# Modulation weights multiplied on VectorE in the gating stage of a two-layer trunk kernel

## The chip, the cores and the metric

The kernel runs on one core of a Trainium2 chip. The metric is the device time of one execution in microseconds (us), lower is better. The engines carry the profile's names: PE is TensorE (matmuls), PEld its weight loads, DVE is VectorE, ACT is ScalarE, POOL is GpSimd, SP is the engine that issues most DMA transfers, in the order of its queue.

## What is computed

A trunk of two layers over 1024 latent tokens and 256 context tokens of width 1024. Layer 0 joins a recurrent branch (RG-LRU) and a spatial gating unit; layer 1 joins a gated convolution and differential attention. Around both stands the adaptive modulation, which the change is about:

```python
def modulation(cond, w, b):
    m = jax.nn.silu(cond) @ w + b                       # w: 1024 x 3072, one for each layer
    shift, scale, gate = jnp.split(m[:, None, :], 3, axis=-1)
    return shift, scale, gate

for l in range(DEPTH):                                  # two layers
    shift, scale, gate = modulation(c, w_mod[l], b_mod[l])                # latent tokens
    shift_c, scale_c, gate_c = modulation(c_ctx[None], w_mod[l], b_mod[l])  # context tokens
    h = x * (1.0 + scale) + shift
    hc = ctx * (1.0 + scale_c) + shift_c
    ...                                                 # y, yc from the layer's branches
    x = layer_norm(DEEPNORM_ALPHA * x + gate * y, ln_g[l], ln_b[l])
    if need_ctx_out:                                    # layer 0 only
        ctx = layer_norm(DEEPNORM_ALPHA * ctx + gate_c * yc, ln_g[l], ln_b[l])
```

There are two conditioning vectors, `c` and `c_ctx`, so each modulation is a product of a 2 x 1024 matrix with a 1024 x 3072 one. The 3072 columns are worked off in six blocks of 512 columns a layer: blocks 0 and 1 are the shift, 2 and 3 the scale, 4 and 5 the gate. The context's gate of layer 1 is not needed.

## The kernel before, in words

Matmuls with f32 accuracy are made of three passes: both operands are split into a high and a low part (`hi`, `lo`; ScalarE makes the first, GpSimd mostly the second), and three of the four products are summed. The kernel goes through these stages, times on the profile's clock:

- **Start** (to about 52 us): shift and scale of layer 0 and the modulated inputs. The change leaves it as it is.
- **Recurrent stage** (to about 232 us): four blocks of 128 channels. `lru_x` and `lru_g` are projections, `lru_rec` the gate matmuls (`pgate`) with ScalarE's activations, `lru_scan` the recurrence on VectorE, whose result goes to DRAM (`ya_d`). The rest of the modulation is done here, in eight blocks: `mod_load` loads eight weight tiles of 128 x 512 (`wm`), and `mod_step`, which stands between the parts of the stage and acts on every third call, does with `mod_do` the sixteen passes of one block (`modp`, L221) and the end of the block before: for shift and scale four transposes (`modcp`, L228) and sums on VectorE (`mod_cols`), for gates one matmul with a column selector (`gatep`, L494), the bias and a store to DRAM (`gate_d`).
- **Gating stage** (to about 367 us): the v projection by ten tiles of 128 tokens (`sgu_v`, tile `pv`) with a normalisation of each on VectorE (`vf`), the spatial matmuls (`sgu_s`, tile `sps`) that take two or three normalised tiles at a time between the matmuls of a later `pv`, and u and z projections of four channel groups (`pu`, `pz`). The first group's z and the second's u come at its beginning, the second group's z after the tiles, and then u and z of the third and of the fourth.
- **Output of layer 0**, then layer 1: projections, attention, output.

Each engine works off its instructions in program order. That order is the kernel's scheduler's, apart from some stretches on SP that are written by hand; a buffer of a pool (`bufs=n`) is given out again when the last reader of its old tile is done, and memory of a pool that was closed goes to later pools under the same condition.

Of the kernel before, what the change touches and what calls it, by code (L numbers as in the profile page):

```python
# [10 lines left out]
F32 = mybir.dt.float32  # L11
# [20 lines left out]
    ("slng", 4), ("slnb", 4), ("lng0", 8), ("lnb0", 8), ("sconv", 12), ("subln", 1), ("sel", 2),  # L32
# [10 lines left out]
def tile_hybrid_trunk(es: ExitStack, tc: tile.TileContext, A, out, scr=None):  # L43
# [48 lines left out]
    V.memset(cm05, -0.5)  # L92
    csil = const.tile([128, KT, 32], F32, name="csil")
# [272 lines left out]
    with pool("lrua") as lp, pool("lruc") as lc:  # L366
# [28 lines left out]
        def lru_g(f):  # L395
            if f:
                p = pj3("pg")
                PROJ(proj3c_g(p, wload(A["w_in0"][4 + f])))
            else:
                p = pg0  # L400
# [5 lines left out]
        def lru_rec(f):  # L406
            (wh, wl), = wload(A["wg"][f], nk=4)
            mod_step()
            xl, xh, xo = XL[f]
            bs = []  # L410
            for d in range(2):
# [22 lines left out]
                mod_step()  # L434
# [28 lines left out]
        def mod_load():  # L463
            if not blocks:
                return
            l, blk = blocks.pop(0)
            wm = {}
            for k in range(8):
                w = lp.tile([128, 512], F32, name="wm", tag="wm", bufs=8)
                SY.dma_start(w, A["w_mod"][l][128 * k:128 * k + 128, 512 * blk:512 * blk + 512])  # L470
                wm[k] = w
            pend.append((l, blk, wm))

        def mod_do():
            if late:
                mod_c(*late.pop(0))
            if pend:
                l, blk, wm = pend.pop(0)
                p = psb("modp")
                mod_mm(p, wm, range(8))  # L480
# [793 lines left out]
```

## Time and profile before

| | us |
|---|---|
| median of three runs | 1142.44 |
| the three runs | 1144.62, 1142.44, 1142.17 |
| the profiled execution | 1142.67 |
| its span in the trace | 1140.8 |
| PE busy | 1117.0 (98%) |
| DVE busy | 721.7 (63%) |
| ACT busy | 435.4 (38%) |
| POOL busy | 285.2 (25%) |
| granted TensorE clock, mean | 0.998 |

All durations below come from the one profiled execution. Its span leaves out 1.9 us around the traced instructions. Busy shares are means over stages with different limits; what an instruction costs is read from its stage, from the engine that is waited for there.

### The profile page before, as it was taken

To read this page: it belongs to the slowest core of one execution; us is meant where nothing else is said; L and a number is where in the kernel's file an instruction comes from. 1 tells how busy PE (TensorE), PEld (TensorE's weight loads), DVE (VectorE), ACT (ScalarE), POOL (GpSimd) and SP (SyncE) were. 2 spreads that over 40 slices of the span, in tenths; PEclk is the share of its full clock that TensorE was granted. 3 is DMA by queue.
4 is the path that set the end of the run, shared out by engine and by line. 5 is a ranking of instruction groups with operands and counts; after the bars stand their busy time and mean duration, and the time that the engine had idled before them with its cause. 6 is when DMAs were issued, how large, how long until landed. Compare 5 with 4: busy or idle time off the path is not lost.

```text
span 1140.8 us, 14960 instructions
## 1 busy us (share of the span) xinstructions
PE 1117.0 (98%) x5842; PEld 920.2 (81%) x5842; DVE 721.7 (63%) x1031; ACT 435.4 (38%) x681; POOL 285.2 (25%) x228
## 2 busy tenths in 40 slices
PE   6999999999999999999999999999999999999997
PEld 4777777878888888888888788888888888888886
DVE  5777986944412566637512776767676666738996
ACT  3463665620221243343212545445544444423210
POOL 0011112630240222258402322322421321220021
PEclk9999999999999999999999999999999999999999
DMA  9644543220241543336736242441522520127641
GB/s 367 258 172 164 185 151 108 94 97 1 75 145 61 174 149 125 114 123 211 240 93 177 96 121 72 114 119 62 144 94 47 137 99 20 47 70 238 217 146 69
DMA packets 78198, 148.08 MB, mean 130 GB/s; under 512 B 6304, under 2 KB 35872, under 8 KB 77232
## 3 DMA queue, kind: packets, MB, share of 16 engines
q1 hardware_dynamic: 71088, 128.25, 32.6%
q0 software_dynamic: 7040, 18.88, 7.4%
q8 instruction: 46, 0.75, 0.3%
q14 instruction: 24, 0.20, 0.1%
HBM read 112.49 MB, written 34.62 MB: 129 GB/s over the span
## 4 chain that ended last, share of the span: by engine, by line
PE 85%; DVE 4%; issue 3%; ACT 3%; POOL 2%; DMA 2%; POOLq 0%; SPq 0%; DVEq 0%; ACTq 0%
PE pout L681 6%; PE pout L683 6%; PE pout L682 6%; PE p L184 5%; PE p L186 5%; PE p L185 5%; PE pv L208 3%; PE pv L210 3%; PE pv L209 3%; PE psc L990 3%; PE psc L991 3%; PE atr L1013 3%; PE modp L221 2%; PE pav L1025 2%; PE pav L1027 2%
## 5 line engine op out<-in xcount | busy, mean ns | idle before, releaser
L141 POOL TENSOR_TENSOR wlo<-wraw,whi 128x512 fp32r<-128x512 f32 x86 | 133.5, 1556 | 427.8 <-ACT whi L138 427.7
L992 DVE TENSOR_REDUCE st<-psc 128x1 f32<-128x1280 f32 x64 | 95.0, 1485 | 39.6 <-PE psc L991 39.6
L681 PE MATMUL pout<-woh,yhi 128*128 128x512 f32 (+1 forms) x296 | 114.7, 387 | 0.1
L683 PE MATMUL pout<-woh,ylo 128*128 128x512 f32 (+1 forms) x296 | 114.4, 386 | 0.0
L682 PE MATMUL pout<-wol,yhi 128*128 128x512 f32 (+1 forms) x296 | 114.1, 385 | 0.0
L994 ACT ACTIVATE e<-psc,st 128x1280 f32<-128x1280 f32 x64 | 85.1, 1330 | 71.9 <-DVE st L992 69.1
L138 ACT ACTIVATE whi<-wraw 128x512 fp32r<-128x512 f32 x92 | 57.4, 627 | 125.1 <-PE px L173 26.9
L184 PE MATMUL p<-hhl,whi 128*128 128x512 f32 x256 | 105.0, 410 | 0.0
L186 PE MATMUL p<-hhl,wlo 128*128 128x512 f32 x256 | 100.5, 393 | 0.0
L185 PE MATMUL p<-hll,whi 128*128 128x512 f32 x256 | 100.3, 392 | 0.0
L138 ACT ACTIVATE ah<-atr 128x512 fp32r<-128x512 f32 (+1 forms) x96 | 47.0, 524 | 64.3 <-PE atr L1013 63.9
L990 PE MATMUL psc<-k,qh 128*128 128x512 f32 (+1 forms) x192 | 67.1, 364 | 2.6 <-ACT e L994 2.5
L991 PE MATMUL psc<-k,ql 128*128 128x512 f32 (+1 forms) x192 | 68.7, 358 | 0.0
L681 PEld LDWEIGHTS pout<-woh,yhi 128*128 128x128 f32 x296 | 55.7, 188 | 11.8 <-DVE zt L644 0.5
L683 PEld LDWEIGHTS pout<-woh,ylo 128*128 128x128 f32 x296 | 55.6, 188 | 11.6 <-DVE ylo L141 0.2
L682 PEld LDWEIGHTS pout<-wol,yhi 128*128 128x128 f32 x296 | 55.7, 188 | 11.4
L138 ACT ACTIVATE yhi<-yraw 128x512 fp32r<-128x512 f32 x36 | 22.5, 631 | 107.7 <-PE pout L682 72.1
L141 DVE TENSOR_TENSOR al<-atr,ah 128x512 fp32r<-128x512 f32 (+1 forms) x96 | 54.4, 593 | 6.3 <-ACT ah L138 6.2
L186 PEld LDWEIGHTS p<-hhl,wlo 128*128 128x128 f32 x256 | 48.0, 188 | 10.8
L185 PEld LDWEIGHTS p<-hll,whi 128*128 128x128 f32 x256 | 48.3, 189 | 8.2
L184 PEld LDWEIGHTS p<-hhl,whi 128*128 128x128 f32 x256 | 48.2, 188 | 8.0
L208 PE MATMUL pv<-wvh,hhl 128*128 128x512 f32 x128 | 52.0, 406 | 0.0
(325 smaller groups left out, 2817.2 us busy)
## 6 DMA issues: line engine op xcount, KB each, us to landing
wraw<-in_w_in_dram SPq DMA_DIRECT2D x42, 512.0 KB, 3.8
wm<-in_w_mod_dram SPq DMA_DIRECT2D x64, 256.0 KB, 4.4
wraw<-in_w_out_dram SPq DMA_DIRECT2D x16, 512.0 KB, 4.4
wm<-in_w_mod_dram SPq DMA_DIRECT2D x7, 1024.0 KB, 11.5
xt<-in_xcT_dram SPq DMA_DIRECT2D x8, 640.0 KB, 8.2
xres<-in_xc_dram SPq DMA_DIRECT2D x10, 512.0 KB, 3.6
wvr<-in_w_v_dram SPq DMA_DIRECT2D x8, 512.0 KB, 3.6
n_d<-xres SPq DMA_DIRECT2D x8, 512.0 KB, 2.6
```

The costliest lines, as they stand in the source:

```text
L138: S.activation(hi, src, AF.Copy)
L141: le.tensor_tensor(lo, src, f32(hi), op=ALU.subtract)
L184: T.matmul(o, hi[:, k % 4], hh[:, k], start=k == 0, stop=False)
L185: T.matmul(o, hi[:, k % 4], hl_[:, k], start=False, stop=False)
L186: T.matmul(o, lo[:, k % 4], hh[:, k], start=False, stop=k == KT - 1)
L208: T.matmul(p, hh[:, k], wh, start=k == 0, stop=False)
L681: T.matmul(o, hi[:, i], wh[:, c], start=first and i == 0, stop=False)
L682: T.matmul(o, hi[:, i], wl[:, c], start=False, stop=False)
L683: T.matmul(o, lo[:, i], wh[:, c], start=False, stop=not first and i == 3)
L990: T.matmul(o, qh[:, m, cu], KS[hd, m][:, c:c + n], start=True, stop=False)
L991: T.matmul(o, ql[:, m, cu], KS[hd, m][:, c:c + n], start=False, stop=True)
L992: V.tensor_reduce(st[:, m:m + 1], p[:, 256:1536], axis=AX.X, op=ALU.max, negate=True)
```

## The change

The whole block of modulation work leaves the recurrent stage. `mod_sums`, a generator, takes its place: for each of the eight blocks it loads the eight weight tiles one by one through three buffers, and VectorE multiplies a tile with the conditioning of its 128 rows (one number per partition), for the two conditioning vectors in turn, and adds it to an accumulator of 128 x 512 (`macc`). A block takes 16 such products, or 8 for the two blocks of which one conditioning is needed: 112 in all, 14 scalings (L237) and 98 multiply-adds (L239). `mod_rows` then lets TensorE sum the accumulator over the partitions: for shift and scale by eight matmuls with a column of ones, one column each (L253), for a gate by one matmul of 512 columns per conditioning (L260). The generator is called forward in the gating stage by `mod_step(n)`, which counts products: 5 (three tiles, six products) in each `sgu_v`, 12 after the second group's z, 14 after each later u and z, and all that is left after the fourth u. The sums of a block are issued when the fourth tile of the next block has been multiplied. One of the six `vf` buffers is given up.

```diff
+    sel = const.tile([128, 3], F32, name="sel")
+    V.memset(sel, 1.0)
+    V.memset(sel[:, 1:2], 0.0)
...
-    sel = P("sel")
-
-    def mod_cols(mb, out, bias, one):
-        p = psb("modcp")
-        for i in range(4):
-            T.transpose(p[:, 128 * i:128 * i + 128], mb[:, 128 * i:128 * i + 128], ident)
-        t = const.tile([128, 4, 2], F32, name="mct", tag="mct", bufs=2)
-        V.tensor_reduce(t, p.rearrange("p (i g r) -> p i r g", g=4, r=32)[:, :, 0:2, :], axis=AX.X, op=ALU.add)
-        for o, i0, i1, b, add in zip(out, (0, 2), (2, 4), bias, one):
-            V.scalar_tensor_tensor(o, t[:, i0:i1, :], add, b[:, :, None].to_broadcast([128, i1 - i0, 2]),
+    def mod_sums(mw):
+        blocks = [(1, i) for i in range(4)] + [(0, 4), (0, 5), (1, 4), (1, 5)]
+        late = None
+        for l, blk in blocks:
+            conds = 1 if (l, blk // 4) == (1, 1) else 2
+            acc = mw.tile([128, 2, 512], F32, name="macc", tag="macc", bufs=2)
+            for k in range(KT):
+                w = mw.tile([128, 512], F32, name="wm", tag="wm", bufs=3)
+                SY.dma_start(w, A["w_mod"][l][128 * k:128 * k + 128, 512 * blk:512 * blk + 512])
+                for c in range(conds):
+                    if k == 0:
+                        V.tensor_scalar(acc[:, c], w, csil[:, k, c:c + 1], None, op0=ALU.mult)
+                    else:
+                        V.scalar_tensor_tensor(acc[:, c], w, csil[:, k, c:c + 1], acc[:, c], op0=ALU.mult, op1=ALU.add)
+                if k == 3 and late is not None:
+                    mod_rows(mw, *late)
+                    late = None
+                yield conds
+            late = (l, blk, acc, conds)
+        mod_rows(mw, *late)
+
+    def mod_rows(mw, l, blk, acc, conds):
+        p = psb("modp")
+        if blk < 4:
+            s, j = divmod(blk, 2)
+            for i in range(4):
+                for c in range(2):
+                    T.matmul(p[:, 2 * i + c:2 * i + c + 1], acc[:, c, 128 * i:128 * i + 128], onesm[:, 0:1],
+                             start=True, stop=True)
+            V.scalar_tensor_tensor(mod1[:, 4 * j:4 * j + 4, s, :], p[:, 0:8].rearrange("p (i c) -> p i c", c=2),
+                                   float(s), P("bmod1")[:, 4 * blk:4 * blk + 4][:, :, None].to_broadcast([128, 4, 2]),
                                    op0=ALU.add, op1=ALU.add)
+        else:
+            for c in range(conds):
+                T.matmul(p[0:2, :], sel[:, c:c + 2], acc[:, c], start=c == 0, stop=c == conds - 1)
+            br = mw.tile([2, 512], F32, name="br", tag="br", bufs=1)
+            SY.dma_start(br, A["b_mod"][l:l + 1, 512 * blk:512 * blk + 512].to_broadcast([2, 512]))
+            V.tensor_tensor(br, p[0:2, :], br, op=ALU.add)
+            SY.dma_start(gate_d[2 * l:2 * l + 2, 512 * (blk - 4):512 * (blk - 4) + 512], br)
 
...
 in lru_x and lru_g:
-                PROJ(proj3c_g(p, WX1 if f == 1 else wload(A["w_in0"][f])))
+                run(proj3c_g(p, WX1 if f == 1 else wload(A["w_in0"][f])))
...
 in lru_rec:
-            mod_step()
 for d in range(2):
-                mod_step()
...
-        def mod_load():
...
-        def mod_do():
...
-        def mod_c(l, blk, mb):
...
-        mod_load()
...
         rec3 = lru_rec(3)
-        while pend or late:
-            mod_do()
...
+    mw_cm = pool("modw")
+    modg = mod_sums(mw_cm.__enter__())
+
+    def mod_step(n):
+        while n > 0:
+            c = next(modg, None)
+            if c is None:
+                return
+            n -= c
+
...
         def sgu_v(t, between=None):
...
             VH[t] = vf
+            mod_step(5)
...
         SY.dma_start(yb_d[1], zt1)
+        mod_step(12)
...
         sgu_u(g, w)
+        mod_step(14)
...
         sgu_z(g, w)
+        mod_step(14 if g == 2 else 100)
```

What moves, at three places. The first is VectorE's order where the v projection begins. `zt` L551 is the z step of the first channel group, L459 the end of the last recurrence, and BN_STATS to `vf` the normalisation of token tiles 0 and 1. Before:

```order
L551 SCALAR_TENSOR_TENSOR zt_1639<-zt_1639,pz 128x1280
L459 SCALAR_TENSOR_TENSOR gt<-gt,sg 128x1024
L579 BN_STATS bs<-vf_1987 128x6
L580 BN_AGGR bs<-bs 128x2
L581 TENSOR_SCALAR bs<-bs 128x1
L583 TENSOR_SCALAR vf_1987<-vf_1987,bs 128x512
L579 BN_STATS bs<-vf_1988 128x6
L580 BN_AGGR bs<-bs 128x2
```

In the changed kernel the rows from the recurrence's end (L488) on are these; line numbers are those of the new file, where the statistics and `vf` are L563 to L567:

```order
L488 SCALAR_TENSOR_TENSOR gt<-gt,sg 128x1024
L237 TENSOR_SCALAR macc<-wm,csil 128x512 x2
L239 SCALAR_TENSOR_TENSOR macc<-wm,csil,macc 128x512 x8
L563 BN_STATS bs<-vf_1717 128x6
L239 SCALAR_TENSOR_TENSOR macc<-wm,csil,macc 128x512 x2
L564 BN_AGGR bs<-bs 128x2
L239 SCALAR_TENSOR_TENSOR macc<-wm,csil,macc 128x512 x2
L565 TENSOR_SCALAR bs<-bs 128x1
L239 SCALAR_TENSOR_TENSOR macc<-wm,csil,macc 128x512 x2
L237 TENSOR_SCALAR macc<-wm,csil 128x512 x2
L567 TENSOR_SCALAR vf_1717<-vf_1717,bs 128x512
L563 BN_STATS bs<-vf_1718 128x6
```

and the rows up to the normalisation of token tile 2 (`vf_1719`), the last that the first spatial matmuls read:

```order
L567 TENSOR_SCALAR vf_1718<-vf_1718,bs 128x512
L590 SCALAR_TENSOR_TENSOR Bt<-rsum,par,Bt 128x128 x2
L239 SCALAR_TENSOR_TENSOR macc<-wm,csil,macc 128x512 x2
L564 BN_AGGR bs<-bs 128x2
L239 SCALAR_TENSOR_TENSOR macc<-wm,csil,macc 128x512 x2
L565 TENSOR_SCALAR bs<-bs 128x1
L239 SCALAR_TENSOR_TENSOR macc<-wm,csil,macc 128x512 x2
L563 BN_STATS bs<-vf_1720 128x6
L567 TENSOR_SCALAR vf_1719<-vf_1719,bs 128x512
```

Thirty products now stand ahead of the normalisation of tile 2. The second place is SP's queue at the same time; the changed kernel has, from the four loads of v weights on:

```order
L199 DMA wvr<-in_w_v_dram 128x2x512 x4
L490 DMA ya_d<-gt 128x256
L270 DMA wraw<-in_w_out_dram 128x1024
L490 DMA ya_d<-gt 128x1024
L544 DMA wsr<-in_sgu_wT_dram 128x512
L546 DMA Bt<-in_sgu_b_dram 128x512
L234 DMA wm<-in_w_mod_dram 128x512 x3
L262 DMA br<-in_b_mod_dram 2x512
```

The first three weight tiles (`wm`) stand behind both stores of the last recurrence. The third is SP's queue at the third and fourth channel groups. Before, from the load of the fourth z's weights to that group's store of its result:

```order
L145 DMA wraw<-in_w_in_dram 128x1024
L239 DMA wraw<-in_w_out_dram 128x1024 x3
L646 DMA yb_d<-zt 128x1280
L722 DMA gc<-gate_d 128x512 x2
L646 DMA yb_d<-zt 128x1280
```

After, from the last two w_out loads of that stretch on:

```order
L270 DMA wraw<-in_w_out_dram 128x1024 x2
L264 DMA gate_d<-br 2x512
L234 DMA wm<-in_w_mod_dram 128x512
L262 DMA br<-in_b_mod_dram 2x512
L632 DMA yb_d<-zt 128x1280
L234 DMA wm<-in_w_mod_dram 128x512
L264 DMA gate_d<-br 2x512
L234 DMA wm<-in_w_mod_dram 128x512 x2
L262 DMA br<-in_b_mod_dram 2x512
L234 DMA wm<-in_w_mod_dram 128x512 x5
L711 DMA gc<-gate_d 128x512
L234 DMA wm<-in_w_mod_dram 128x512 x2
```

Here the rest of the weight tiles, the bias rows (`br`), the stores of the gate rows and the loads of the context's gate (`gc`) stand in one queue. On TensorE the last two gate sums stand between the fourth group's u and z:

```order
L175 MATMUL pu<-hhl,whi 128x512
L176 MATMUL pu<-hll,whi 128x512
L177 MATMUL pu<-hhl,wlo 128x512
L260 MATMUL modp<-macc,sel 2x512 x2
L175 MATMUL pz<-hhc,whi 128x256
L176 MATMUL pz<-hlc,whi 128x256
L177 MATMUL pz<-hhc,wlo 128x256
```

Nothing stood between these two projections before.

## Rows read from the trace of the kernel before

**Rows 1.** The page: busy time by engine, and the shares of the chain of waits

```profile
PE 1117.0 (98%) x5842; PEld 920.2 (81%) x5842; DVE 721.7 (63%) x1031; ACT 435.4 (38%) x681; POOL 285.2 (25%) x228
...
PE 85%; DVE 4%; issue 3%; ACT 3%; POOL 2%; DMA 2%; POOLq 0%; SPq 0%; DVEq 0%; ACTq 0%
```

**Rows 2.** Timeline of PE, recurrent stage: start us, us, engine, line, operation, tiles, shape, count

```profile
63.48 1.92 PE L221 MATMUL modp<-wm,csil 128*32 128x512 f32 x16
65.34 0.50 PE L172 MATMUL px<-hhl,whi 128*128 128x512 f32 x1
...
77.60 0.59 PE L494 MATMUL gatep<-mb,par 128*2 128x512 f32 x1
...
80.27 0.38 PE L172 MATMUL pg<-hhc,whi 128*128 128x256 f32 x1
...
114.53 0.60 PE L228 MATMUL modcp<-ident,mb 128*128 128x128 f32 x4
...
116.91 0.38 PE L419 MATMUL pgate<-xh,whi 128*128 128x258 f32 x1
...
191.84 0.29 PE L419 MATMUL pgate<-xh,whi 128*128 128x258 f32 x1
...
203.43 1.02 PE L494 MATMUL gatep<-mb,par 128*2 128x512 f32 x2
204.38 0.39 PE L172 MATMUL pz<-hhc,whi 128*128 128x256 f32 x1
```

**Rows 3.** Timeline of ACT, second channel block; in brackets the idle time and its releaser

```profile
118.97 1.34 ACT L423 ACTIVATE gt<-pgate,hb 128x1282 f32<-128x1282 f32 x1 [0.84 <-PE pgate L421]
```

**Rows 4.** Timelines of DVE and PE around the start of the gating stage

```profile
231.22 1.48 DVE L551 SCALAR_TENSOR_TENSOR zt<-zt,pz 128x1280 f32<-128x1280 f32 x1
232.62 2.16 DVE L459 SCALAR_TENSOR_TENSOR gt<-gt,sg 128x1024 f32<-128x1024 f32 x1
...
232.75 0.51 PE L208 MATMUL pv<-wvh,hhc 128*128 128x512 f32 x1 [0.60 <-DVE zt L551]
```

**Rows 5.** Timeline of PE later in the kernel, at a sum over partitions

```profile
691.85 0.95 PE L1039 MATMUL pms<-onesm,sq 128*128 128x1 f32 x8
692.66 0.48 PE L184 MATMUL p<-hhl,whi 128*128 128x512 f32 x1
```

**Rows 6.** Timeline of PE, first group of spatial matmuls

```profile
257.32 0.83 PE L591 MATMUL sps<-wsr,vf 128*128 128x128 f32 x6
```

**Rows 7.** Groups of DVE by line and form: busy us, mean ns | idle before

```profile
L732 DVE SCALAR_TENSOR_TENSOR xres<-xres,pout 128x512 f32<-128x512 f32 x20 | 13.7, 683 | 1.2 <-DMA xres<-in_xc_dram 0.8
...
L579 DVE BATCH_NORM_STATS2 bs<-vf 128x6 f32<-128x512 f32 x10 | 6.9, 694 | 27.2 <-ACT vf L577 27.2
L583 DVE TENSOR_SCALAR vf<-vf,bs 128x512 f32<-128x512 f32 x10 | 5.4, 545 | 5.0 <-POOL bs L582 4.9
```

**Rows 8.** Windows: busy us of PE, PEld, DVE, ACT, POOL; PEclk, DMA share, GB/s

```profile
260.00:280.00 20.00, 20.00 (x101) 16.69 (x101) 7.21 (x17) 1.79 (x3) 1.64 (x3) 1.00 0.00 0
1137.00:1138.00 1.00, 0.00 (x0) 0.00 (x0) 0.43 (x1) 0.00 (x0) 0.00 (x0) 0.50 0.36 141
```

**Rows 9.** Tile wm: us from issue to landing, 73 loads of all sizes

```profile
DMA to landing us min/median/max: 2.7/4.5/13.6
```

**Rows 10.** Timelines of SP's queue and of PE, third and fourth channel groups

```profile
332.62 9.76 SPq L239 DMA_DIRECT2D wraw<-in_w_out_dram  x3
...
350.60 3.04 SPq L722 DMA_DIRECT2D gc<-gate_d  x2
...
339.62 0.28 PE L172 MATMUL pu<-hhc,whi 128*128 128x256 f32 x1
...
353.36 0.28 PE L172 MATMUL pz<-hhc,whi 128*128 128x256 f32 x1
```

**Rows 11.** Timeline of PE at the start of the kernel, recurrent input projections

```profile
11.59 1.31 PE L164 MATMUL px<-hhl,whi 128*128 128x512 f32 x2
...
21.02 0.63 PE L164 MATMUL px<-hhl,whi 128*128 128x512 f32 x2
```

More of the change, by code (lines that the diff above doesn't have):

```diff
@@ L31 @@
     ("cc", 16), ("bmod0", 24), ("bmod1", 24), ("convw", 16), ("convb", 4), ("ba", 8), ("bx", 8), ("lam", 8),
-    ("slng", 4), ("slnb", 4), ("lng0", 8), ("lnb0", 8), ("sconv", 12), ("subln", 1), ("sel", 2),
+    ("slng", 4), ("slnb", 4), ("lng0", 8), ("lnb0", 8), ("sconv", 12), ("subln", 1),
 ]
@@ L397, in lru_g @@
                 p = pj3("pg")
-                PROJ(proj3c_g(p, wload(A["w_in0"][4 + f])))
+                run(proj3c_g(p, wload(A["w_in0"][4 + f])))
             else:
@@ L461, in lru_scan @@
                 SY.dma_start(ya_d[f][:, s0:s0 + n], y[:, c0:c0 + n])
-        def mod_load():
[L464 to L472, printed above, removed]
-        def mod_do():
[L475 to L480, printed above, removed]
-                mb = lp.tile([128, 512], F32, name="mb", tag="mb", bufs=1)
-                V.tensor_copy(mb, p)
-                late.append((l, blk, mb))
-                mod_load()
-        def mod_c(l, blk, mb):
-            if blk < 4:
-                s, j = divmod(blk, 2)
-                k0 = 4 * j
-                mod_cols(mb, [mod1[:, k0 + 2 * i:k0 + 2 * i + 2, s, :] for i in range(2)],
-                         [P("bmod1")[:, 4 * blk + 2 * i:4 * blk + 2 * i + 2] for i in range(2)], (float(s),) * 2)
-            else:
-                pg = psb("gatep")
-                T.matmul(pg[0:2, :], sel, mb, start=True, stop=True)
-                br = lp.tile([2, 512], F32, name="br", tag="br", bufs=1)
-                SY.dma_start(br, A["b_mod"][l:l + 1, 512 * blk:512 * blk + 512].to_broadcast([2, 512]))
-                V.tensor_tensor(br, pg[0:2, :], br, op=ALU.add)
-                SY.dma_start(gate_d[2 * l:2 * l + 2, 512 * (blk - 4):512 * (blk - 4) + 512], br)
-        blocks = [(0, 4), (0, 5)] + [(1, i) for i in range(6)]
-        late, pend, calls = [], [], [0]
-        def mod_step():
-            calls[0] += 1
-            if calls[0] % 3 == 2:
-                mod_do()
-        def interleave(gen):
-            for i, _ in enumerate(gen):
-                if i in (9, 17):
-                    mod_step()
-        PROJ = interleave
-        mod_load()
         lru_x(0)
@@ L534, in tile_hybrid_trunk @@
         rec3 = lru_rec(3)
-        while pend or late:
-            mod_do()
     vp_cm = pool("sguv", side="right")
@@ L562, in tile_hybrid_trunk @@
         SY.dma_start(Bt, A["sgu_b"].rearrange("g p -> (g p)")[None, :].to_broadcast([128, 512]))
-        VF = [vw.tile([128, 512], F32, name=f"vf{i}") for i in range(6)]
+        VF = [vw.tile([128, 512], F32, name=f"vf{i}") for i in range(5)]
         so_cm.__exit__(None, None, None)
@@ L575, in sgu_v @@
                 run(between)
-            vf = VF[t % 6]
+            vf = VF[t % 5]
             S.activation(vf, p, AF.Gelu_apprx_tanh)
@@ L663, in tile_hybrid_trunk @@
         sgu_z(g, w)
+        mod_step(14 if g == 2 else 100)
     gp_cm.__exit__(None, None, None)
+    mw_cm.__exit__(None, None, None)
     pj_cm.__exit__(None, None, None)
@@ L1219, in pack @@
         "subln": cols(a["diff_subln_g"][0]),
-        "sel": (np.arange(128)[:, None] % 32 == np.arange(2)[None]).astype(f),
     }
```

## The prediction, made before the change was run

> **What bounds the kernel now.** I read the page's busy shares and the shares of the chain of waits first. TensorE (PE) is busy 1117.0 us of a span of 1140.8 and carries 85% of the chain [rows 1]; no other engine is busy more than 63%. So time taken off TensorE shortens the run, time put on it lengthens it, and work on VectorE (DVE) is free until TensorE has to wait for it. Next I read TensorE's timeline in the two stages that the change touches, and asked at each step which engine TensorE needs next. In the recurrent stage (to about 232) the modulation stands in the middle of TensorE's stream [rows 2]. In the gating stage TensorE has no gap while VectorE is busy 7.21 us in 20 and the DMA share is 0.00 [rows 8]. That looks like room for 112 products, but it is an average: the products stand in VectorE's program order ahead of operations that TensorE waits for, and each needs a weight tile that is loaded through three buffers. I therefore look for the two places where TensorE reads something that comes after them.
>
> **What the change removes.** From the start of one step to the start of the next, modulation takes 1.86 us of TensorE once (63.48 to 65.34), 2.67 us with the two-pass gate sum ahead of it (77.60 to 80.27; three places), 2.38 us with the four transposes (114.53 to 116.91; four places) and 0.95 us for the last gate sum (203.43 to 204.38) [rows 2]. Sum 1.86 + 3 x 2.67 + 4 x 2.38 + 0.95 = 20.3 us. Of these 2.67 + 0.95 come after 191.84, where the fourth block's gate matmuls begin; 16.7 us lie ahead of it. Not all of that is gained. Some steps stood between gate matmuls while ScalarE drained their sums: in the second block ScalarE was idle 0.84 us before the sum behind the 2.38 us step [rows 3], so of that 2.38 only 0.84 is sure. Lost in the same way over three blocks could be 0 to 4.6 us; I take 1.5, since that spacing is the tight one, and the fourth block's gate matmuls begin 15.2 us earlier. The 3.6 us after that are hidden: TensorE then waits for VectorE's z step of the first channel group (L551) before the v projection [rows 4]. The new order puts that step ahead of the last three of the recurrence. I count 1.0 us for it (0 to 4; whatever it gives beyond, the first wait below takes back, since it ends with VectorE and not with TensorE). Start of the v projection: **-16.2 us**. The 64 weight loads and the VectorE steps that leave the recurrent stage hid under TensorE and count nothing.
>
> **What it adds on TensorE.** Four blocks of eight matmuls with one column: four such, in eight passes, took 0.81 us (691.85 to 692.66) [rows 5], so 1.62 each, 6.5 us. Six gate matmuls of 512 columns at 0.95 us, as the old gate sum [rows 2]: 5.7 us. Together **+12.2 us**. With nothing else the run would gain 4.0 us.
>
> **The first wait.** From here times stand on the old profile's clock, as if the fourth block's gate matmuls still began at 191.84. VectorE's last step of the recurrence ended at 232.62 + 2.16 = 234.8 [rows 4]; with the z step moved ahead of it I take 237 (234.5 to 237.5). In SP's new order the first weight load stands behind both stores of that result and its buffer lies in memory that they still read. A store and then a load each take at least 2.7 us, with a median of 4.5 [rows 9]; since these queues are otherwise empty here, DMA share 0.00 a little later [rows 8], I take 2.7 for the store and 3.3 for the load. The first product starts at 243. In VectorE's order 30 products stand ahead of the last normalisation that the first spatial matmuls need (vf of token tile 2): 4 scalings at 0.545 us (L583) and 26 multiply-adds at 0.683 (L732) [rows 7], 19.9 us. With them stand four statistics at 0.694, three normalisations at 0.545 [rows 7] and ten small steps, an estimated 2 us: 26.4 in all. An operation started 0.08 us before the end of the one ahead (231.22 + 1.48 against 232.62 [rows 4]); over 47 steps that takes off up to 3.7. I take 25, so vf is ready at 268. TensorE starts the v projection at 231.75, reaches the first spatial matmuls 257.32 - 232.75 = 24.6 us later [rows 4, 6], and does one new sum of 1.6 on the way: 257.9. **Wait 10.1 us.** Short values all along (234.5, 2.7, 2.7, 22.7) give 262.6 and 4.7; a load at the median and three buffers that then set the pace give about 15. After this VectorE has per token tile 6 products and some 2.3 us of its own work, about 6.3 us, against TensorE's 6; the lag is used up by the new sums, and I count no further wait in this part.
>
> **The second wait.** The last gate sums stand between u and z of the fourth channel group, so TensorE waits there for all 64 products. Let Z be the end of the third group's z projection (339.62 in the old trace). On SP, the last w_out load went out at 332.62 + 9.76 = 342.38, Z + 2.8 [rows 10]; behind it now stand the store of a gate row, which waits for TensorE's gate sums and VectorE's addition, and then tile 51. I take Z + 4.6 for it. Each tile needs the buffer of the third tile before: 51, 54, 57, 60, 63 are five rounds, one after the other, of a load (3.0), a product (0.68) and an issue (about 0.4), 4.1 us, so the last product ends at Z + 25.1. TensorE gets there at Z + 4 x 0.95 + 13.74 (339.62 to 353.36 [rows 10]) + 0.95 = Z + 18.5. **Wait 6.6 us.** It can't be much under 3.5: between tiles 59 and 60, and again between 61 and 62, SP now holds a load of the context's gate row into a weight buffer of the fourth u, and in the old trace SP stood at these until 350.60 and 353.6, 11.0 and 14.0 us after u began [rows 10]. With u beginning at Z + 3.8 and two more loads behind the second, that gives Z + 22. With loads of 4.4 the rounds give Z + 30.5, a wait of 12.
>
> **The clock after a wait.** At the start of the kernel, after standing idle, two matmuls of 512 columns took 1.31 us at 11.59, and 0.63 at 21.02 [rows 11]: half pace. [...] So two idle stretches of this length may each be followed by matmuls at half pace; the pace came back somewhere between the two; I take 4.4 us at half pace, of which 2.2 are lost, after each wait: **+4.4 us** (0 to 7). [...]
>
> **Sum**, on the profiled run's 1142.67 us (0.2 over the median, so the two are not told apart): -16.2 + 12.2 + 10.1 + 6.6 + 4.4 = +17.1, **1160 us**. Behind the gating stage TensorE bounds each stage, so nothing gives the time back.
>
> **The rivals.**
> *The first wait is small* (2 us or less): VectorE takes the products faster than the nearest rows, or the first loads go out before the stores land. For it: VectorE's idle time there. Against it: the order of VectorE's and SP's rows. 1142.67 - 16.2 + 12.2 + 1 + 6.6 + 2.2 = 1148.5.
> *The loads are slow*: landing at the median of 4.4 to 4.5, as in the recurrent stage, makes both waits long: 15 and 12. 1142.67 - 16.2 + 12.2 + 15 + 12 + 4.4 = 1170.
> *Not slower: VectorE keeps ahead of the first spatial matmuls*, because the weight loads run some 10 us ahead of what I assume and vf of tile 2 is ready by 257.9. Then the first wait is gone, the second is at its floor of 3.5, and the clock doesn't fall: 1142.2; without the second also, 1138.7. It decides at a sum of waits and clock of 4.0 us. For it speaks VectorE's busy share of a third in that stretch [rows 8]; against it that the 30 products are 20 us and stand behind VectorE's step that ends at 237.
> *The change doesn't take off what it says*, since ScalarE sets the recurrent stage's pace: then -12 instead of -16.2, +4 on each of these; it is inside the range.
>
> **How the numbers follow.** Both waits, 1160 (its own range 1152 to 1167): 0.60. Small first wait, 1148.5: 0.13. Slow loads, 1170: 0.16. Not slower: 0.11, of which 0.06 is faster. The range goes down to the small first wait and up to just under the slow loads: 1148 to 1169. A difference of 0.2%, 2.3 us, is about what can be told from no change: faster 0.06, same 0.05, slower 0.89.
>
> **What would show it.** In the new trace: the fourth block's gate matmuls near 176.6; the first product some 10 us after the v projection begins; a gap before the first spatial matmul, of about 10 us, put down to VectorE's vf; multiply-adds of 0.6 to 0.7 us; a second gap of 4 to 12 us before the last gate sums, with VectorE idle for the weight loads meanwhile; and matmuls at half pace after each gap. Wrong would be: no gap in front of the spatial matmuls, loads that land before 232, or products much under 0.6 us.

## The result: 3.3% slower, more than twice the forecast loss

The changed kernel takes 1180.37 us (median of 4 runs, 1179.03 to 1182.77) against 1142.47 (1142.17 to 1144.62): a ratio of 1.033, with a 95% interval of 1.0317 to 1.0343. The profiled execution took 1179.95, its span is 1178.2 against 1140.8 before, +37.4 us. The forecast was +17.1, in a range that ended at 1169.

From the profile page of the changed kernel: busy time by engine, and the chain of waits.

```profile
PE 1118.3 (95%) x5766; PEld 927.1 (79%) x5766; DVE 794.3 (67%) x1129; ACT 435.1 (37%) x681; POOL 291.0 (25%) x228
...
PE 72%; DVE 10%; DMA 8%; ACT 5%; issue 3%; POOL 1%; SPq 1%; POOLq 0%; DVEq 0%; ACTq 0%
```

TensorE is as busy as before [rows 1], but its part of the chain fell from 85% to 72%. VectorE and DMA have what it lost. Where TensorE waits for them, from 218 us to 520, is in the changed kernel's waits: who waits for whom, us in total, times, longest.

```profile
PE modp L260 <- DVE macc L239: 16.7, 2, 9.9
PE sps L576 <- DVE Bt L590: 4.6, 1, 4.6
PE sps L576 <- DVE vf L567: 3.9, 1, 3.9
PE pout L670 <- ACT woh L141: 2.3, 1, 2.3
PE pv L211 <- ACT ut L553: 1.5, 1, 1.5
PE pv L211 <- DVE zt L525: 1.3, 1, 1.3
PE pout L671 <- DVE wol L144: 0.8, 1, 0.8
```

Both waits are where the forecast put them: ahead of the first spatial matmuls (L576) and at the last gate sums (L260). The first is near its size, the second 2.5 times too long. (The first comes in two parts; `Bt`, L590, stands in VectorE's order right behind the normalisation of token tile 1.) TensorE's timeline in the changed kernel shows them in place (columns as in [rows 2], the wait in brackets).

```profile
176.41 0.29 PE L449 MATMUL pgate<-xh,whi 128*128 128x258 f32 x1
...
218.23 0.50 PE L211 MATMUL pv<-wvh,hhc 128*128 128x512 f32 x1 [1.32 <-DVE zt L525]
...
251.10 1.19 PE L576 MATMUL sps<-wsr,vf 128*128 128x128 f32 x4 [4.62 <-DVE Bt L590]
256.15 0.80 PE L576 MATMUL sps<-wsr,vf 128*128 128x128 f32 x2 [3.86 <-DVE vf L567]
...
345.23 0.59 PE L260 MATMUL modp<-macc,sel 128*2 128x512 f32 x1
...
369.58 1.86 PE L260 MATMUL modp<-macc,sel 128*2 128x512 f32 x2 [6.79 <-DVE macc L239]
381.38 1.87 PE L260 MATMUL modp<-macc,sel 128*2 128x512 f32 x2 [9.93 <-DVE macc L239]
383.17 0.58 PE L175 MATMUL pz<-hhc,whi 128*128 128x256 f32 x1
...
398.10 0.39 PE L670 MATMUL pout<-woh,yhi 128*128 128x512 f32 x1
```

The fourth block's gate matmuls begin 15.4 us earlier than in [rows 2], the v projection 14.5 us earlier than in [rows 4]. The windows of the changed kernel (columns as in [rows 8]) show the price of that:

```profile
240.00:250.00 10.00, 6.47 (x37) 5.22 (x35) 10.00 (x23) 0.60 (x1) 1.98 (x2) 0.95 0.55 163
250.00:260.00 10.00, 5.04 (x19) 4.22 (x20) 10.00 (x22) 0.00 (x0) 0.99 (x1) 0.54 0.45 136
...
300.00:320.00 20.00, 20.00 (x127) 17.92 (x127) 19.18 (x27) 5.24 (x7) 5.40 (x4) 1.00 0.50 156
...
340.00:350.00 10.00, 10.00 (x42) 5.90 (x41) 4.99 (x7) 2.00 (x3) 0.86 (x1) 1.00 0.61 210
370.00:380.00 10.00, 1.44 (x2) 0.00 (x0) 6.26 (x9) 0.00 (x0) 0.00 (x0) 0.50 0.78 230
```

VectorE (third number) has no room left where it had two thirds [rows 8]: 10.00 of 10 and 19.18 of 20 us. From 340 to 350 it starves, busy 4.99 of 10, and the last 13 tiles go out only after that. What it starves for is in the queue of SP, and ahead of that on ScalarE (ACT) and GpSimd (POOL); timelines of the changed kernel:

```profile
328.14 0.33 SPq L613 DMA_DIRECT2D yb_d<-zt  x1
...
329.63 11.65 SPq L234 DMA_DIRECT2D wm<-in_w_mod_dram  x5
341.38 0.38 SPq L148 DMA_DIRECT2D wraw<-in_w_in_dram  x1
...
351.57 5.74 SPq L270 DMA_DIRECT2D wraw<-in_w_out_dram  x2
357.36 0.28 SPq L264 DMA_DIRECT2D gate_d<-br  x1
357.76 0.33 SPq L234 DMA_DIRECT2D wm<-in_w_mod_dram  x1
...
348.00 1.06 ACT L141 ACTIVATE woh<-wraw 128x1024 fp32r<-128x1024 f32 x1 [11.53 <-DMA wraw<-in_w_out_dram]
...
351.49 5.47 POOL L144 TENSOR_TENSOR wlo<-wraw,whi 128x512 fp32r<-128x512 f32 x2
```

The third z projection ends at 345.23, the Z of the prediction. Tile 51 goes out at 357.76, Z + 12.5. The forecast had Z + 4.6. Up the queue: SP stood at five tile loads for 11.65 us; 8.4 of these it waited for VectorE to give back a buffer, 2.0 for an earlier load. The w_in load behind them left at 341.38 (before at 328.87), ScalarE got its w_out tile at 348.00, and GpSimd's part of the splits, to 356.96, held the last two w_out loads until 357.31. The gate row's store and tile 51 stand behind those.

### The profile page after: what moved, and what is told of

Read it like the earlier page. It is cut to its first block, busy times and chain, and to the rows that moved or that the text cites. A ratio compares the mean times of both kernels' runs of the same rounds, so it can differ in the third digit from the quotient of the medians.

```text
span 1178.2 us, 14942 instructions
## 1 busy us (share of the span) xinstructions
PE 1118.3 (95%) x5766; PEld 927.1 (79%) x5766; DVE 794.3 (67%) x1129; ACT 435.1 (37%) x681; POOL 291.0 (25%) x228
## 4 chain that ended last, share of the span: by engine, by line
PE 72%; DVE 10%; DMA 8%; ACT 5%; issue 3%; POOL 1%; SPq 1%; POOLq 0%; DVEq 0%; ACTq 0%
PE pout L672 5%; PE pout L671 5%; PE pout L670 5%; PE p L187 4%; PE p L188 4%; PE p L189 4%; PE psc L979 3%; PE psc L980 3%; PE atr L1002 3%; DVE macc L239 3%; DMA wm<-in_w_mod_dram 3%; PE pv L211 3%; PE pv L213 3%; PE pv L212 3%; PE pav L1014 1%
## 5 line engine op out<-in xcount | busy, mean ns | idle before, releaser
L144 POOL TENSOR_TENSOR wlo<-wraw,whi 128x512 fp32r<-128x512 f32 x86 | 139.1, 1621 | 446.7 <-ACT whi L141 445.7
L239 DVE SCALAR_TENSOR_TENSOR macc<-wm,csil,macc 128x512 f32<-128x512 f32 x98 | 75.5, 807 | 9.2 <-DMA wm<-in_w_mod_dram 9.1
L672 PEld LDWEIGHTS pout<-woh,ylo 128*128 128x128 f32 x296 | 56.1, 190 | 12.4 <-DVE ylo L144 1.2
L189 PEld LDWEIGHTS p<-hhl,wlo 128*128 128x128 f32 x256 | 48.1, 188 | 10.7
```

The source lines that it names most:

```text
L144: le.tensor_tensor(lo, src, f32(hi), op=ALU.subtract)
L189: T.matmul(o, lo[:, k % 4], hh[:, k], start=False, stop=k == KT - 1)
L239: V.scalar_tensor_tensor(acc[:, c], w, csil[:, k, c:c + 1], acc[:, c], op0=ALU.mult, op1=ALU.add)
L672: T.matmul(o, lo[:, i], wh[:, c], start=False, stop=not first and i == 3)
```

## The experiments

The theory after the result: VectorE's amount of work, not only its order, makes both waits; the second grows because the backlog holds SP's queue. Times are beside 1142.5 for the kernel before; differences are to 1180.4 unless said. Each kernel ran once unless said; the changed kernel's four runs lie 3.7 us apart, and smaller differences are read from the traces alone.

**What the removal is worth alone: the kernel before and the changed one, each without modulation.**

```diff
-        blocks = [(0, 4), (0, 5)] + [(1, i) for i in range(6)]
+        blocks = []
...
# the other kernel
-    modg = mod_sums(mw_cm.__enter__())
+    modg = iter(())
...
```

> The kernel before with the eight blocks of modulation left out (constants in their place) and everything else, the memory of each stage too, as it was. The changed kernel without its modulation took 1133.9, since 4.3 us came back in the output stage, where its loads of the residual and of the gates go out only after the gating stage. Theory (the new pool takes the memory into which these loads could go early): here they go out early again, there is no wait in the output stage and the whole gain stays: 1128.5 us (1127 to 1130). Rival (the removal itself brings the wait, since the output stage comes nearer to its loads): 1132 to 1135.

> Leaves out the modulation of the second layer and all gates altogether (no weight loads, no products, no sums; constants stand in their place), so it times the removal alone. In the changed kernel the v projection starts 14.5 us earlier than before (218.2 against 232.8). If everything else in its loss is waits and sums that the products bring, this kernel keeps those 14.5 us to the end: 1128 us (1125 to 1130). If part of the loss is something else (the output stage's own waits, code that is laid out in another way), it ends above 1131.

Measured 1128.31 and 1133.94. So the removal is worth 14.2 us. The other 5.6 belong to the second kernel's layout: from the first output matmul to the first of the k projection it takes 123.27 us, 4.3 more than before. Its waits, with those in the gating stage:

```profile
PE pout L675 <- ACT woh L141: 1.5, 1, 1.5
...
PE pv L211 <- ACT ut L558: 1.1, 1, 1.1
PE pout L676 <- DVE wol L144: 1.0, 2, 0.8
```

The two pout waits aren't there in the first. No product runs in either, so the products aren't the cause. In the changed kernel the loads of the output stage's residual and gate rows go out at 403 to 409, ahead of the w_out loads; in the kernel before, at 308 to 310. The loss goes with how late the w_out loads leave behind them. Over all 18 kernels here: where they leave 7.3 to 9.1 us after the first output matmul, the stage takes 119.0 to 120.1 us; where they leave 9.5 to 11.8 us after it, 122.5 to 124.9. Why the loads of the residual moved is not shown; the new pool's place in memory is one possible reason, and the one run on it (below) doesn't decide it. The wait for `ut` (1.1) isn't the products' either, and the first kernel, whose v projection begins as early (217.65), hasn't got it.

**The first wait: fewer products ahead of it, no loads, another order.** The first 15 tiles left out; then all products reading one resident tile:

```diff
...
+                if n[0] > 15:
                     w = mw.tile([128, 512], F32, name="wm", tag="wm", bufs=3)
# the other kernel
-                SY.dma_start(w, A["w_mod"][l][128 * k:128 * k + 128, 512 * blk:512 * blk + 512])
+                w = wres
...
```

> Leaves out the loads and products of the first 15 weight tiles, those that stand on VectorE ahead of the normalisation of token tile 2; all sums on TensorE stay. Theory: the first wait (8.5 us at the spatial matmuls, and 3 us at half pace behind it) goes and the second stays at 16 to 17 us: 1168 us (1165 to 1171). Rival (one backlog, which the first tiles build up and the last sums pay for): the second wait shrinks as well, under 1158.

> Leaves out the 63 other weight loads: all 112 products read one resident tile, so VectorE's work and order are unchanged and SP's queue is free of weight tiles. Theory (the second wait is SP's queue, 16.7 us; the first is VectorE's order, about 10): the second wait is gone, the first is under 4 us since the products can begin before the stores of the last recurrence have landed; 1145 us (1141 to 1149). Rival (VectorE's time for 112 products is the cause of both waits): still above 1158.

Measured 1169.75 and 1165.97. The first is as expected. The second misses its 1145 by 21 us and lies above its rival's 1158. Without the 15 tiles, the waits of that kernel hold none for VectorE at the spatial matmuls, and the second is as it was:

```profile
PE modp L265 <- DVE macc L244: 16.5, 2, 9.9
```

Without loads a wait of the first one's size stays, now at the first block's sums ahead of the spatial matmuls (L254), and the second (L261) falls to 2.6:

```profile
PE modp L254 <- DVE macc L240: 8.6, 1, 8.6
...
PE modp L261 <- DVE macc L240: 2.6, 1, 2.6
```

The first product still stands behind one load and starts at 230.06, and 32 products stand ahead of the normalisation of tile 2. So the first wait is the products' own time, and the second needs the loads. Besides its waits in the gating stage this kernel has the sums (12.2) and loses 5.8 us in the output stage.

Then the order. One tile a step instead of five, with the rest and the last sums later; VectorE's order in the stage fixed as written; and that with the last sums later:

```diff
-            mod_step(5)
+            mod_step(1 if t < 3 else 5)
...
# the other two
+        dv_cm = tc.manual_schedule(engines={nc.vector.engine})
+        dv_cm.__enter__()
...
```

> Same work, two changes of pace: one weight tile instead of three at each of the first three token tiles (the six go to the second z and the third u and z), and the last six tiles with the two last sums behind the fourth z. Theory (the first wait is the number of products ahead of the normalisation of tile 2; the second is where the last sums stand): first wait under 3 us, last sums wait 2 to 6 us as in the run with the late sums alone (3.6): 1152 us (1148 to 1157). Rival (what is not done early is missing late): first wait gone but the third z to the output stage wait more, 1160 or above.

> Same work; VectorE's order from the first token tile to the store of the second group's result is the program's, written by hand, so that the products of a token tile stand behind its own normalisation: 12 products and not 30 stand ahead of the normalisation of tile 2, and the second group's z steps no longer wait behind products. (Calling fewer products forward had changed nothing, since the scheduler puts them as early as it can.) Theory (the first wait is this order; the second begins with VectorE's late z step, whose store holds up SP's queue): no wait at the first spatial matmuls (-8.5 and -3 at half pace), the second wait 8 to 13 instead of 16.7: 1163 us (1158 to 1169). Rival (the amount of VectorE's work counts, and not its order): the time comes back at the sums of the first blocks or at the last sums, 1174 or above.

> The order of the run before and, as well, the last six tiles and the two last sums behind the fourth z. Theory: no first wait, the last sums wait 0 to 4 us: 1151 us (1147 to 1156). What is left over the kernel before would be the sums on TensorE (12 us) and the output stage's waits, less the 14.5 us of the recurrent stage. Rival (the two waits are one backlog): 1158 or above.

Measured 1168.59, 1184.89, 1165.41. All three miss their forecast (1152, 1163, 1151) and lie beyond the bound of their rival (1160, 1174, 1158). In the first, the scheduler put the same 30 products ahead of the spatial matmuls, whatever was written, and the wait there grew:

```profile
PE sps L576 <- DVE vf L567: 13.7, 4, 5.8
```

In the second they were spread as written. The one wait became five of 0.3 to 2.5 us, 7.7 together, and from the v projection's start to the second group's z the stage took 82.96 us, against 81.82 in the changed kernel and 63.77 before. The last sums waited 12.4 us, within the 8 to 13 expected, but 5.7 came new at the first layer's gate sums; the third kernel waited 5.5 there, and none at the last. So a mere reordering doesn't give the time back: VectorE's amount of work counts.

**The second wait: moving the sums, or its suspected causes one by one.** The last six tiles and the last sums behind the fourth z:

```diff
-        mod_step(14)
+        mod_step(14 if g == 2 else 6)
```

> Same work; the last six weight tiles and the two sums of the second layer's gate come after the fourth group's z instead of after its u, 13.9 us later on TensorE. Theory (the last product is held up by SP's queue and ends some 36 us after the third z, plus one or two rounds for the tiles that now wait longer): the wait shrinks from 16.7 to 4 to 10 us and much of the slow pace goes: 1169 us (1164 to 1174). Rival (the wait moves along with the sums, since the loads behind are held up by what z needs): 1177 or more.

It took 1162.71 us, 17.7 less and better than both expectations: 3.6 us of the second wait are left, and the output waits are gone from its list. The gating stage gave back 13.8 us, the output stage 3.5. The kernel with fixed order gained as much (1184.89 to 1165.41). Then that kernel had its modulation pool opened after the gating stage's pool (4 runs):

```diff
-    mw_cm = pool("modw")
-    modg = mod_sums(mw_cm.__enter__())
     gp_cm = pool("sgu")
...
```

> The run before with the weight tiles' memory placed behind the gating stage's sums instead of ahead of them, so that less of the output stage's memory waits for the end of the gating stage. Theory (the output stage's loss of 4.3 us is memory that comes free late): 1 to 4 us less than the run before, 1148 us (1144 to 1153), with the loads of the residual going out earlier. Rival (these loads are held up by the gate rows that they need, whatever the memory): within 1 us of the run before.

It took 1168.05 us (1166.87 to 1169.1), a ratio of 1.0219 (1.0202 to 1.0236) to the kernel before: no gain. It doesn't test the theory, though. The kernel it was built on took 120.10 us in the output stage, 1.1 more than the kernel before, so there were no 4.3 us to win; and the residual's loads still left behind the fourth z, at 394. Next come four weight buffers; and then the loads of tiles 35 to 50 left out:

```diff
-                w = mw.tile([128, 512], F32, name="wm", tag="wm", bufs=3)
+                w = mw.tile([128, 512], F32, name="wm", tag="wm", bufs=4)
# the other kernel
+                if not 35 <= n[0] < 51:
...
```

> Four buffers for weight tiles instead of three (paid with one of the buffers for normalised tiles). Theory (rounds through the buffers and loads queued behind one another set the second wait): it shrinks from 16.7 to 8 to 13 us, the first wait stays at 8 to 9: 1174 us (1170 to 1178). Rival (the number of buffers does not matter, the late start does): within 1.5 us of 1180.4.

> Leaves out the loads of weight tiles 35 to 50, which stand in SP's queue among the loads of w_out and of the fourth group's weights; their products read tile 34, so VectorE's work is unchanged. Theory (these tiles held up the w_out loads, and these in turn tile 53 and later ones): the last two w_out loads go out 2 to 5 us after the third z instead of 6 to 12, and the second wait falls from 16.7 to 2 to 8 us, 1167 us (1163 to 1172). Rival (only the rounds of the last tiles matter): the second wait stays above 12.

They took 1180.61 and 1176.56 us. A fourth buffer bought nothing, as its rival had it: tile 51 went out ahead, at 345.21, but the next one only at 361.19. Without those loads but with their products, the last w_out load still ended at Z + 8.2 (Z + 12.1 in the changed kernel), so the loads in the middle alone aren't the cause. The last waits, 12.7 us, are as its rival had them, but say less, since the products that read tile 34 kept its buffer: tile 53 left at 360.73, right behind the last of them. Then the products there were taken away as well, tiles 30 to 50:

> Leaves out the loads of tiles 30 to 50 and their products (all but the first of each block), that is, VectorE's extra work and SP's extra loads during the second z and the third u and z; the last 13 tiles are as in the changed kernel. It tests the step of the prediction that let tile 51 go out 4.6 us after the third z. Theory (the late start, 12.5 us after it, came from VectorE's backlog by way of SP's queue; the rounds of the last tiles are 4.1 to 4.7 us each as predicted): the last w_out load goes out 2 to 4 us after the third z, tile 51 at 4 to 7, the second wait is 6 to 10 us: 1169 us (1165 to 1173). Rival (the last 13 tiles among the gate rows cost this much wherever they start): the second wait stays above 13, 1176 or above.

It took 1167.56 us, in the range expected. SP's queue in that kernel, where Z is 345.47:

```profile
334.52 13.22 SPq L274 DMA_DIRECT2D wraw<-in_w_out_dram  x3
349.30 0.25 SPq L268 DMA_DIRECT2D gate_d<-br  x1
349.70 0.33 SPq L238 DMA_DIRECT2D wm<-in_w_mod_dram  x1
```

The gate row's store leaves at Z + 3.8 and the tile load behind it at Z + 4.2: the prediction's Z + 4.6 for this place in the queue holds once these loads and products are away. The wait is 5.2 us. That it is near the forecast's 6.6 says less: the load at 349.70 is tile 53's, since with buffers free tiles 51 and 52 had left at 284.02 and 285.87, and 11 tiles were to come instead of 13. No run took the products alone away and kept the loads. What is left is how the backlog gets into the queue. Two things there wait for VectorE: the tile loads, and the store of the second group's gated result (L613). The store was moved to ScalarE's queue, the tile loads to GpSimd's, then both; and the store in the kernel without loads.

```diff
-        SY.dma_start(yb_d[1], zt1)
+        S.dma_start(yb_d[1], zt1)
...
# tile loads
-                SY.dma_start(w, A["w_mod"][l][128 * k:128 * k + 128, 512 * blk:512 * blk + 512])
+                G.dma_start(w, A["w_mod"][l][128 * k:128 * k + 128, 512 * blk:512 * blk + 512])
```

> The stores of the first two groups' results go out from ScalarE's queue instead of SP's; everything else as in the changed kernel. Theory (the second group's z step, late on VectorE behind products, holds up SP's queue through its store, and the w_out load behind it): the w_out load behind the store goes out some 5 us earlier, and the second wait falls by 3 to 8 us: 1174 us (1170 to 1177). Rival (the weight tiles in SP's queue, which wait for VectorE themselves, hold it up as much): within 2 us of 1180.4.

> All weight tiles are loaded from GpSimd's queue instead of SP's. Theory (SP's shared queue sets the second wait): the loads of w_out and of the fourth z's weights no longer stand behind tiles that wait for VectorE, and the second wait falls under 10 us; the first wait stays, since it is VectorE's order: 1171 us (1164 to 1177). Rival (whatever queue the tiles stand in, an engine's own work stands behind them; here GpSimd's splits of the weights): new waits on weights in the u and z projections, 1182 or above.

> The tile loads are issued from GpSimd's queue and the stores of the first two channel groups' gated result from ScalarE's queue, both at once. Z is the end of the third group's z projection. Theory, two gates in SP's queue: what VectorE releases late stands ahead of the w_out loads in two ways, the tile loads and the store, and either alone keeps them back, so that moving one alone gave 1180.3 and 1182.6. With both away the last w_out load and the gate row's store behind it go out by Z + 5 (353.3, Z + 6.4, with the tile loads alone moved; Z + 12.1 in the changed kernel), the two last waits fall from 14.6 to about 9 together, and the time is 1172 to 1176. Rival, the backlog works through VectorE and GpSimd themselves (splits that come late because their engines are taken): the gate row's store stays at Z + 6 or later, the time within 2 us of 1180.3.

> The products read one resident tile, so 63 of the 64 loads are left out, and the stores of the first two groups' gated result go out from ScalarE's queue. No tile load and no store that VectorE holds back then stands on SP ahead of the w_out loads. Theory, two gates in SP's queue: with the loads alone left out the store was still there, and the gate row's store went out at Z + 7.9; now it goes out by Z + 5, the last wait falls from 2.6 to under 1.5, and the time from 1166.0 to 1163 to 1165. Rival, the engines themselves: the gate row's store stays at Z + 7 or later, and the time is within 1 us of 1166.0.

Measured 1182.61, 1180.28, 1177.63 and 1161.69. Neither move alone shortened the run: the first two times are within the changed kernel's own runs. Without loads, moving the store does. SP's queue and GpSimd's split of the w_out tile, with the store in SP's queue (Z = 346.75), then with the store moved (Z = 346.95):

```profile
329.02 0.33 SPq L614 DMA_DIRECT2D yb_d<-zt  x1
329.44 0.38 SPq L271 DMA_DIRECT2D wraw<-in_w_out_dram  x1
...
344.71 9.84 SPq L271 DMA_DIRECT2D wraw<-in_w_out_dram  x3
354.60 0.28 SPq L265 DMA_DIRECT2D gate_d<-br  x1
...
335.65 6.54 POOL L144 TENSOR_TENSOR wol<-wraw,woh 128x1024 fp32r<-128x1024 f32 x1 [9.40 <-ACT woh L141]
```

```profile
326.62 0.33 SPq L271 DMA_DIRECT2D wraw<-in_w_out_dram  x1
...
337.29 11.95 SPq L271 DMA_DIRECT2D wraw<-in_w_out_dram  x3
350.79 0.25 SPq L265 DMA_DIRECT2D gate_d<-br  x1
...
331.33 2.52 POOL L144 TENSOR_TENSOR wol<-wraw,woh 128x1024 fp32r<-128x1024 f32 x1 [4.73 <-ACT woh L141]
```

The gate row's store goes from Z + 7.9 to Z + 3.8, the last wait is gone, and 4.3 us come back. The queue is not the whole way, however. The next w_out loads leave 7.4 us earlier (337.29 for 344.71): the split before them begins 4.3 us earlier and takes 4.0 us less, 2.52 for 6.54, and the splits after it lose 0.9 again. The long one stood beside VectorE's products (last section). So the rival, the engines themselves, has a part in it. With loads kept and both moved, the outcome lies between the two expectations: the row's store leaves at Z + 5.9 (352.79, Z = 346.85), and 13.0 us of the second wait remain. The tile loads now stand in GpSimd's queue; ScalarE's part of a w_out tile and GpSimd's queue in that kernel:

```profile
323.13 1.06 ACT L141 ACTIVATE woh<-wraw 128x1024 fp32r<-128x1024 f32 x1 [2.99 <-DMA wraw<-in_w_out_dram]
...
324.89 0.55 POOL L234 DMA_DIRECT2D wm<-in_w_mod_dram  x1 [1.11 <-DVE macc L239]
325.45 2.42 POOL L144 TENSOR_TENSOR wol<-wraw,woh 128x1024 fp32r<-128x1024 f32 x1
```

ScalarE is done at 324.19, and GpSimd's split of the tile starts at 325.45, behind a tile load that waited 1.11 us for VectorE. So the backlog acts through this in-order queue too. How much of the 13.0 us comes that way was not separated.

No kernel tried that does the whole work beats the one before. By the first pair the most to be had is 14 us, and the sums on TensorE take 12 of that back.

## Why the prediction was right in sign and wrong in size

Its terms, in us, and what the traces show:

| term | forecast | measured |
|---|---|---|
| start of the v projection | -16.2 | -14.5 |
| sums and gate matmuls on TensorE | +12.2 | +12.2 |
| first wait | +10.1 | +9.9 (4.6 + 3.9 + 1.5 for ut) |
| second wait | +6.6 | +16.7 |
| half pace after the waits | +4.4 | +6.0 (by difference) |
| output stage | 0 | +4.6 |
| after it | 0 | +1.8 |
| sum | +17.1 | +36.7, of a span of +37.4 |

**Right.** The recurrent stage gave 15.4 us for the 15.2 counted. The sums over partitions took 1.70 each for 1.62 forecast, the first layer's four gate matmuls 3.53 for 3.8; the last two, at full pace, are counted at their 1.9. The first wait is VectorE's program order, as the changed kernel's timeline shows:

```profile
231.12 0.88 DVE L237 TENSOR_SCALAR macc<-wm,csil 128x512 f32<-128x512 f32 x2 [8.32 <-DMA wm<-in_w_mod_dram]
...
255.56 0.54 DVE L567 TENSOR_SCALAR vf<-vf,bs 128x512 f32<-128x512 f32 x1
```

From the first product to the end of the normalisation that TensorE waits for, 256.10, are 25.0 us, the forecast's 25. The product starts 12.9 us after the v projection; the forecast had 11.25. The forecast's 2.7 us for a store were an estimate from loads [rows 9]; here the first weight load left at 228.40, 5.6 us after the last store at 222.83, and 3.4 of these it waited for that store. The 1.5 us for `ut` in the table stand at 225.47, ahead of the products; without them TensorE would have reached the spatial matmuls that much earlier and waited there instead. TensorE's half pace came where expected, by the granted clock: 0.54 in 250 to 260 and 0.50 in 370 to 380. The 4.4 us at half pace after each wait, and the 2.2 lost of them, were the author's estimate, and no run shows that term; what the changed kernel shows is this: after the first wait, matmuls of 512 columns took 0.63 us from 257.18 to 258.45 and 0.39 at 260.19, 4.04 us after its end at 256.15; after the second those of 256 columns took 0.41 from 383.56 to 385.26 and 0.28 from 385.63 on, 4.25 us after its end at 381.38. By difference, each cost about 3.0 us instead of 2.2: after the first, 18.05 us of growth in that part less three sums (5.1) and 9.9 of waits; after the second, 1.8 in the last sums and 1.2 in the fourth z (14.93 for 13.75).

**Wrong, the main step: "I take Z + 4.6 for it."** Tile 51 went out at Z + 12.5. The 2.8 of the last w_out load was read from a queue that VectorE didn't hold up. The prediction had noted that VectorE would need 6.3 us a tile for TensorE's 6, and asked only whether TensorE would wait there. It didn't. But the lag didn't go away with the new sums; it showed at the store at L613 (4.9 us after the third u began before, 317.00 and 312.14, and 10.7 after, 328.14 and 317.47) and to tile loads that wait for buffers. The gate row's store, which stands right ahead of tile 51, left at Z + 12.1 here, at Z + 7.9 with the products but no loads, and at Z + 3.8 without the loads and products of tiles 30 to 50. So the error came in at this step, and both VectorE's lag and the tile loads have a part in it. Of the 10.1 us too few, 7.9 are the late start (2.9 of these in GpSimd's pair of splits at 351.49, 5.47 us, where the pair at this place took 2.56 before) and 3.0 the rounds, which took 4.7 us each instead of 4.1 (357.76 to 381.3 for five); 0.9 goes off again, since the gate sum between the two waits ran at half pace meanwhile.

**Wrong: "nothing gives the time back", with no cost behind the gating stage.** The output stage lost 4.6 us, and the kernel without modulation loses 4.3 of it in the same place, where the w_out loads leave late behind the residual's loads. Who reads the order of loads could have seen that the residual's loads had moved behind the fourth z. Why they moved was not settled, and the 1.8 us behind the output stage were not traced to a cause.

**Wrong, small:** the 1.0 us for the z step moved ahead. The v projection still waits 1.32 us for it, where it waited 0.60 [rows 4], and 0.9 us were lost there instead. The slow-load case has a slip in its sum: five rounds of 4.4, 0.68 and 0.4 end at Z + 32.0, not Z + 30.5, a wait of 13.5. Only that rival uses it.

**The rivals.** The small first wait was kept off by the 30 products, and "not slower" fails for the same reason. "The loads are slow" came nearest in time (1170), but by another mechanism: a late start makes most of the excess of the second wait, the tiles landed after 2.7 us in the median, and the first wait stayed near its forecast. The rival that the change doesn't take off what it says had 12 us at the start; 14.5 came.

## What to carry to other kernels

VectorE, busy 7.21 us in 20 [rows 8], had less room here than that number says, since entries that wait for it stood in in-order queues ahead of urgent ones: the gate row's store left SP's queue at Z + 12.1, and at Z + 3.8 without the loads and products of tiles 30 to 50. So list, for each queue, the entries that wait for the engine that gets the work and what is behind them, and cost the lag there, even where the critical engine doesn't wait. Sums that need the last of a long stream belong behind the last work that doesn't need them; here that alone was worth 17.7 us. And compare the kernel without the moved work in both layouts: it splits the price of the work from that of the layout.

## What the runs showed of the hardware

Some of VectorE's products took longer beside GpSimd's splits. In the changed kernel the 98 multiply-adds average 807 ns; the 79 with no GpSimd operation beside them took 0.72 to 0.75 us, and five of the others 1.77 to 2.49, each of which began 0.3 to 0.9 us after a split had begun. Three others that overlapped a split took 0.73 to 0.74. Two rows of the same time, VectorE's and GpSimd's:

```profile
314.03 1.79 DVE L239 SCALAR_TENSOR_TENSOR macc<-wm,csil,macc 128x512 f32<-128x512 f32 x1
...
313.77 1.49 POOL L144 TENSOR_TENSOR wlo<-wraw,whi 128x512 fp32r<-128x512 f32 x1 [12.95 <-ACT whi L141]
```

The split ends at 315.26 and the product at 315.82, 0.56 us later, most of the 0.72 to 0.75 that a product took alone; the other four ended as long, 0.54 to 0.55 us, after their split. The kernel without loads shows the reverse. VectorE's operations beside the split at 335.65 that took 6.54 us:

```profile
330.49 8.03 DVE L240 SCALAR_TENSOR_TENSOR macc<-wm,csil,macc 128x512 f32<-128x512 f32 x12
338.45 1.48 DVE L624 TENSOR_TENSOR ss<-ss,ut 128x1280 f32<-128x1280 f32 x1
```

They follow one another without a gap to 339.93, the products at 0.67 us each, and the split ends 2.3 us after them, about the 2.4 that such a split took in the changed kernel at 334.96. With the store moved, the split at 331.33 took 2.52, and twelve such products from 330.85 on, beside this split and the next ones, took 14.42 us. Why one or the other is slowed was not shown, and one pair isn't settled: the splits at 351.49 took 5.47 us in the changed kernel and 2.54 in the kernel without loads, in the same place and beside much the same VectorE operations.
